# A two-block transformer kernel on one Trainium2 core: its on-chip pools are created in another order, so that the weights and the large tiles start at multiples of 2048 bytes

## The chip, the cores and the metric

The kernel runs on one core of one Trainium2 chip. The core has a matrix engine (TensorE, "PE" in the profile, with its weight loads shown apart as "PEld"), a vector engine (DVE), a scalar engine (ACT), GpSimd (POOL) and SyncE (SP), which here only starts transfers. They work from SBUF, an on-chip memory of 128 partitions; TensorE writes its sums to PSUM. The metric is the device time of one execution in microseconds.

## The reference, cut to what matters

256 tokens of width 1024 pass through two blocks of two layers each. The first block's layer is a gated feed-forward, a mixer of four kinds of attention, and another gated feed-forward; the second block's layer is a mixer of three kinds of attention and one gated feed-forward, with norms that are modulated by a vector c.

```python
def swiglu(h, w_gate, w_up, w_down):
    return (jax.nn.silu(h @ w_gate) * (h @ w_up)) @ w_down

for l in range(DEPTH):                                   # first block
    x = x + 0.5 * swiglu(rms_norm(x, ffn1_norm[l]), ffn1_w_gate[l], ffn1_w_up[l], ffn1_w_down[l])
    h = rms_norm(x, mix_norm[l])
    parts = split_in_proj(h @ w_in[l])
    ...                                                  # o_a, o_b, o_c, o_d: four kinds of attention
    x = x + jnp.concatenate([o_a, o_b, o_c, o_d], axis=-1) @ w_out[l]
    x = x + 0.5 * swiglu(rms_norm(x, ffn2_norm[l]), ffn2_w_gate[l], ffn2_w_up[l], ffn2_w_down[l])

for l in range(DEPTH):                                   # second block
    h = rmsnorm(x, g_mix_pre[l]) * (1.0 + scale_a) + shift_a
    y = hybrid_mixer(h, w_in[l], ...)
    x = x + gate_a * rmsnorm(y, g_mix_post[l])
    h = rmsnorm(x, g_ffn_pre[l]) * (1.0 + scale_f) + shift_f
    x = x + gate_f * rmsnorm(swiglu_2(h, w_gate_up[l], w_down[l]), g_ffn_post[l])
```

Everything is float32, and the large products have to be about that exact.

## The kernel before

**Products in three parts.** A float32 product a·b is made of three products of TensorE's type float32r: a is split into a high and a low part, and so is b, and ah·bh + ah·bl + al·bh is summed in PSUM (`mm3`, line 607). In a product the stationary operand, which a weight load brings into the array first, is 128 tokens of activations (128x128), and the moving operand is 512 columns of the weights (128x512). So every product of 512 columns has a weight load of its own, and three products in a row (a *triple*) make one exact step.

**Weights.** `WStream` (line 378) reads the weights in units of 128x2048 floats (8 KB in each partition): a transfer brings a unit into a tile `raw` (three slots), ACT copies it to `whi` (which rounds it), and DVE subtracts to get `wlo` (four slots each). Both are used once for each of the two tiles of 128 tokens.

**Activations.** `xh` and `xl` hold the transposed, normed input of a phase, 8 KB each in a partition, for the whole phase. The products of the input projections and of gate and up read them as their stationary operand and write the PSUM tile `mm`: in the profile they are `mm<-whi,xh`, `mm<-wlo,xh` and `mm<-whi,xl`. The products of the down projection read the gated middle, transposed and split into `hth` and `htl`, and write the PSUM tiles `y`: `y<-whi,hth`, `y<-wlo,hth`, `y<-whi,htl`. The output projection of a mixer is the same with `oth` and `otl`. These four, and all the small tiles of attention, live in slots of 2 KB of one pool (`m`, line 591, 20 slots). `proj` (line 612) runs through the triples of one `mm` tile, `down` in `ffn` through those of `y`.

**Order.** The program is recorded by `Plan`, and a list schedule with a table of costs sets the order in which each engine takes its instructions. Addresses play no part in that schedule. Every recorded instruction is issued from line 304, so the profile shows one line for nearly all of them, and they are told apart by their tiles.

**Places in SBUF.** A tile pool takes the next free bytes of every partition when it is created, in units of 32 bytes. The pools are created in `Net.__init__`: first `const`, `keep`, `row`, `big` and `sm`, which hold tiles of all sizes, then `mid` (the 2 KB slots), `raw` and `w`. `x`, `xh` and `xl` are tiles of `keep`.

Of the kernel before, what the change touches and what calls it, by code (L numbers as in the profile page):

```python
# [11 lines left out]
F32 = mybir.dt.float32  # L12
F32R = mybir.dt.float32r
# [18 lines left out]
# order of the output projections' (token tile, group of 256 columns); pools of attention's PSUM beside them  # L32
# [3 lines left out]
# engines of the copies out of PSUM, in turn  # L36
COPY = "a"
# the first two units come in CUTS pieces, FIRST of them before the second token tile; up to NCUT in two;
# splits of the others in SPLITS pieces
CUTS, FIRST, NCUT, SPLITS = 4, 2, 5, 2  # L40
# products that warm the array's clock while the first loads are under way
WARM = 8
# the list schedule
# [4 lines left out]
class Pool:  # L48
    """A tile pool whose tiles the plan knows: which slots they share and how many there are."""
# [23 lines left out]
class Plan:  # L73
    """Records the program in its order, then issues it in the order of a list schedule:
    every engine takes, of the instructions whose operands are there, the one needed soonest."""
# [72 lines left out]
    def cost(self, eng, method, args, kw, aps):  # L148
        """ns on the engine, ns on the DMA rings, activation table."""
        if method == "dma_start":  # L150
            return (1000 if eng == "gpsimd" else 475), 4 * int(np.prod(list(args[0].shape))) / 360, None
        n = max(int(np.prod(list(a.shape)[1:])) for k, a in aps)
        psum = any(a.space == PSUM for _, a in aps)
        if eng == "tensor":
            if method == "transpose":
                return 109, 0, None
            n = kw["rhs"].shape[-1]
            if kw["rhs"] is self.cold:
                return 4 * max(107, n / 1.2 + 2), 0, None
            if kw["rhs"].dtype == F32R:  # L160
                return n / 2.4 + 2.5, 0, None
            return 2 * max(107, n / 1.2 + 2), 0, None
        if eng == "scalar":
            extra = 93 * sum(1 for k, _ in aps if k in ("bias", "scale", "accum_out"))
            f = args[2] if len(args) > 2 else kw.get("func")
            return 0.833 * n + (52 if psum else 94) + extra, 0, "silu" if f == AF.Silu else "exp" if f in (AF.Exp, AF.Ln) else None
        if eng == "vector":
            fast = method in ("tensor_copy", "tensor_scalar", "memset") and not psum
            scalars = sum(1 for k, _ in aps if k not in (0, 1, "out", "in_")) if method == "tensor_scalar" else 0
            scalars += sum(1 for k, _ in aps if k == 2) if method == "scalar_tensor_tensor" else 0  # L170
            return n * (0.52 if fast else 1.042) + 68 + 62 * scalars, 0, None
        if eng == "gpsimd":
            if kw.get("op") == ALU.pow:
                return 300 + 165 * n, 0, None
            return 148 + (3.15 if method == "tensor_copy" else 2.11) * n, 0, None
        return 60, 0, None

# [1 line left out]
    def order(self, prio):  # L179
        """List schedule: every engine starts, of what can start within DELTA of the soonest, the most urgent.  # L180
        A tile may take a slot before its turn if the program's order could still go on from there."""
# [41 lines left out]
        def slot_time(i):  # L223
            """When the slots of the tiles that op i touches first are free; None: not now."""
# [81 lines left out]
    def priorities(self):  # L306
        """How long before the end an op has to start, by a schedule from the end; no later than LATE behind
        the large products it was recorded with, and the first loads in their order."""
# [15 lines left out]
    def backward(self, start):  # L324
        """List schedule from the end; a tile waits for the one that had its slot in the program's order."""
# [52 lines left out]
class WStream:  # L378
    """Weights in the order of their use: load ahead, split into hi + lo float32r parts ahead."""
# [9 lines left out]
    def cuts(self, i, n):  # L389
        """The first units come in pieces: the products start the sooner."""  # L390
        k = CUTS if i < 2 else 2 if i < NCUT else 1
        return [slice(j * n // k, (j + 1) * n // k) for j in range(k)]
# [10 lines left out]
    def _load(self, pieces=None):  # L403
        """The next unit, or only the next pieces of it."""
# [47 lines left out]
class Net:  # L452
    def __init__(self, ctx, tc, A, out, stop):
# [3 lines left out]
        pool = lambda name, bufs=1, **k: Pool(nc, ctx.enter_context(tc.tile_pool(name=name, bufs=bufs, **k)), bufs)  # L457
        self.const = pool("const")
        self.keep = pool("keep")
        self.row_p = pool("row", 3)  # L460
        self.big = pool("big", 1)
        self.sm = pool("sm", 4)
        self.mid_p = pool("mid", NMID)
        self.ps = pool("ps", 2, space=PSUM)
        raw_p = pool("raw", 3)
        w_p = pool("w", WStream.BUFS)
        self.ident = self.const.tile([P, P], F32, name="ident")
        self.mhalf = self.const.tile([P, 64], F32, name="mhalf")
        self.x = [self.keep.tile([P, D], F32, name=f"x{t}") for t in range(2)]
        self.xh = self.keep.tile([P, 8, S], F32R, name="xh")  # L470
        self.xl = self.keep.tile([P, 8, S], F32R, name="xl")
# [61 lines left out]
    def rstd2(self, ss):  # L533
        """(ss[0] + ss[1] + eps) ** -0.5: the two halves' parts of a mean of squares."""
# [6 lines left out]
    def norm(self, t, gain, shift=None):  # L541
        """rms_norm(x_t) * gain (+ shift)"""
# [18 lines left out]
    def first_xT(self, t, gain):  # L561
        """xh/xl columns of token tile t := transpose of x_t * gain; the tokens' factors come after the products."""
# [28 lines left out]
    def m(self, n, name, dt=F32):  # L591
        """One of the shared 2 KB slots."""
        return self.mid_p.tile([P, 512], dt, tag="m", name=name)[:, :n]
# [15 lines left out]
    def proj(self, ps, n, t, half, u, kts=4):  # L609
        """ps[128, n] += x^T k-tiles of one weight unit [128, kts, n]."""  # L610
# [125 lines left out]
    def slot(self):  # L736
        """Between the products of a feed-forward: one step of the work that block 2 needs early."""
        if self.bg and next(self.bg[0], self) is self:
            self.bg.pop(0)
# [10 lines left out]
    def copy(self, out, in_):  # L750
        """PSUM -> SBUF, on the engines in turn."""
# [6 lines left out]
    def consts1(self):  # L758
# [4 lines left out]
        self.rope1 = C.tile([P, 2, 176], F32, name="rope1")  # L763
# [15 lines left out]
    def skew(self, name, src, offset, nh, rows, n):  # L779
        """Every head's n values once per row, each row SKEW after the one before: read at SKEW - 1 they slide."""  # L780
# [5 lines left out]
    def diff_lambda(self, l):  # L786
        """-lambda on every partition; the output gain times (1 - lambda_init)."""
# [17 lines left out]
    def na_bias(self, l):  # L805
        """8 * (relative bias, or -1e30 outside the window), [token of a tile, tile, head, key]."""
# [19 lines left out]
    def prep(self, t, ps, segs, w, rope, dstT, flag):  # L826
        """Heads' norms, gains and rotations of a [128, n] projection, then its transpose."""
# [54 lines left out]
    def job(self, kind, l, h, q, k, vh, col, bias=None):  # L882
        """softmax(q k / 8 + bias) v for one head, both token tiles of queries."""
# [32 lines left out]
    def turn_p(self, p):  # L916
        """[query, (tile, key)] -> [key of a tile, (query tile, key tile, query)]"""
# [54 lines left out]
    def turn_o(self, g, flag):  # L972
        """o columns of one group of 256, transposed and split for the output projection."""
# [135 lines left out]
    def modulation(self):  # L1109
        """Rows of block 2's norms: gain * (1 + scale), shift, gate * post gain, twice per layer."""  # L1110
# [52 lines left out]
    def t5_bias(self):  # L1163
        """8 * (table[bucket(q - k)], or -1e30 above the diagonal), keys of the tile before | own tile."""
# [34 lines left out]
    def gated_residual(self, t, y, i):  # L1199
        """x_t += gate * rms_norm(y) * gain"""  # L1200
# [11 lines left out]
    def rot2(self, X, nh, t):  # L1212
        """Rotary positions on [128, nh, 32]."""
# [7 lines left out]
    def latents(self, l, t, ps, st):  # L1221
        """Norms of the latents and their transposes, rotated shared key, forget logits."""
# [27 lines left out]
    def forget(self, l, st):  # L1250
        """F, the cumulative log forget gates: min(z, 0) - log(1 + e), e = exp(-|z|), log(1 + e) = 2 artanh(e / (2 + e)); the fox biases 8 * (F[q] - F[k]), or -1e30 above the diagonal."""
# [26 lines left out]
    def qk_fox(self, t, ps, dst, st):  # L1278
        """Queries [q, 8 F, 1] and keys [k, 1, -8 F], transposed: their products are 8 (q k / 8 + F[q] - F[k])."""
# [32 lines left out]
    def latent_heads(self, t, ps, part, st):  # L1312
        """Four heads of the up-projections: queries (part 0) or keys and values (part 1), transposed."""
# [22 lines left out]
    def causal_job(self, kind, q, k, vh, col, bias, scale):  # L1336
        """Causal softmax(q k * scale + bias) v for one head; bias comes divided by the scale."""
# [30 lines left out]
    def group_norm(self, l, g0, ng):  # L1368
        """rms_norm over groups g0 .. of 256 columns of o, then transposed, times the gain, and split."""
# [188 lines left out]
def pack(inputs):  # L1558
    """Weights laid out as the units are read: every partition's part of a unit is contiguous."""
# [52 lines left out]
def shape_consts():  # L1612
    """Positions, masks and multiplicities: functions of the shapes alone."""
# [51 lines left out]
```

## Time and profile before

| | us |
|---|---|
| three runs | 1671.84, 1675.52, 1676.18 |
| median | 1675.52 |
| span of the profiled execution, first to last instruction | 1670.4 |
| PE busy in it | 1646.5 (99%) |
| PEld, DVE, ACT, POOL busy | 1346.0 (81%), 1086.1 (65%), 841.8 (50%), 166.3 (10%) |

The profiled execution has no time of its own beside its span; the span lies 5.1 us below the median of the three runs. PE's busy time overlaps itself, since matmuls are pipelined: a product of 512 columns is shown as about 0.39 us long, and the next one starts some 0.23 us after it. So what a product costs in a stream is read from the distance between two starts, and not from its length.

### The profile page before, as it was taken

What the parts mean: (1) busy time and instruction counts of PE and PEld (TensorE: products, weight loads), DVE (VectorE), ACT (ScalarE), POOL (GpSimd) and SP (SyncE); (2) the same over time, 40 slices, a digit from 0 to 9 for tenths busy, and PEclk for the clock granted to TensorE, in tenths of its full rate; (3) what the DMA queues carried; (4) which work ended last, traced back from release to release, by engine and by line L of the source; (5) the groups of instructions that cost most, each with busy time, mean ns of one, the idle gap of its engine ahead of it and who ended that gap; (6) DMA issues with size and microseconds to landing.
All of it is one profiled execution on the core that took longest, in us unless ns stands there. A gap on an engine that the chain in (4) does not pass through costs nothing.

```text
span 1670.4 us, 21333 instructions
## 1 busy us (share of the span) xinstructions
PE 1646.5 (99%) x7912; PEld 1346.0 (81%) x7912; DVE 1086.1 (65%) x1956; ACT 841.8 (50%) x1384; POOL 166.3 (10%) x205
## 2 busy tenths in 40 slices
PE   9989999999999999999999999999999999999998
PEld 7868877888888888887788888888888888888886
DVE  6557788577677776777857655656754476585553
ACT  6544456554444444446554444576643358664442
POOL 0000056000000000026500000120000012000000
PEclk9999999999999999998999999999999999999999
DMA  8587762257776877763328645541655445255451
GB/s 302 210 272 274 262 224 102 76 212 298 271 270 250 306 266 268 288 221 121 127 86 316 229 171 192 173 174 51 239 181 199 150 167 202 96 181 190 171 201 51
DMA packets 81884, 335.78 MB, mean 201 GB/s; under 512 B 17136, under 2 KB 19700, under 8 KB 50676
## 3 DMA queue, kind: packets, MB, share of 16 engines
q1 hardware_dynamic: 81780, 334.42, 55.7%
q8 instruction: 62, 1.02, 0.2%
q14 instruction: 42, 0.34, 0.1%
HBM read 333.29 MB, written 2.84 MB: 201 GB/s over the span
## 4 chain that ended last, share of the span: by engine, by line
PE 94%; DVE 2%; POOL 2%; DMA 1%; ACT 1%; issue 0%; SPq 0%; POOLq 0%; DVEq 0%; ACTq 0%
PE mm L304 55%; PE y L304 27%; PE att L304 6%; PE tp L304 6%; DMA raw<-in_gu 1%; POOL rs L304 1%; DVE wlo L304 1%; POOL qk L304 0%; POOL rot L304 0%; DVE o L304 0%; DVE qk L304 0%; DVE ms L304 0%; DMA t5t<-in_t_table 0%; ACT xh L304 0%; DVE qkT L304 0%
## 5 line engine op out<-in xcount | busy, mean ns | idle before, releaser
L304 DVE TENSOR_TENSOR wlo<-raw,whi 128x1024 fp32r<-128x1024 f32 (+2 forms) x516 | 607.5, 1211 | 273.9 <-ACT whi L304 272.4
L304 ACT CAST whi<-raw 128x1024 fp32r<-128x1024 f32 (+2 forms) x516 | 512.5, 1035 | 319.3 <-PE mm L304 132.3
L304 PE MATMUL mm<-whi,xh 128*128 128x512 f32 (+2 forms) x1376 | 552.5, 402 | 2.8 <-ACT whi L304 1.8
L304 PE MATMUL mm<-wlo,xh 128*128 128x512 f32 (+2 forms) x1376 | 543.2, 395 | 0.2 <-DVE wlo L304 0.2
L304 PE MATMUL mm<-whi,xl 128*128 128x512 f32 (+2 forms) x1376 | 539.6, 393 | 0.8 <-DVE xl L304 0.8
L304 PEld LDWEIGHTS mm<-whi,xl 128*128 128x128 f32 x1376 | 259.5, 189 | 61.4 <-DVE xl L304 1.8
L304 PEld LDWEIGHTS mm<-whi,xh 128*128 128x128 f32 x1376 | 259.5, 189 | 61.4 <-ACT whi L304 2.1
L304 PEld LDWEIGHTS mm<-wlo,xh 128*128 128x128 f32 x1376 | 259.7, 189 | 55.3 <-DVE wlo L304 0.9
L304 PE MATMUL y<-whi,htl 128*128 128x512 f32 x528 | 207.5, 393 | 0.0
L304 PE MATMUL y<-wlo,hth 128*128 128x512 f32 x528 | 207.2, 392 | 0.0
L304 PE MATMUL y<-whi,hth 128*128 128x512 f32 x528 | 207.2, 394 | 0.0
L304 ACT ACTIVATE sil<-mm 128x256 f32<-128x256 f32 x110 | 42.3, 384 | 224.1 <-PE mm L304 223.3
L304 POOL TENSOR_TENSOR rs<-rs,mhalf 128x1 f32<-128x1 f32 x28 | 26.1, 932 | 1286.2 <-DVE rs L304 1286.2
L304 DVE CUSTOM_DVE_ANT_0 ada<-ada,act 128x512 f32<-128x512 f32 x192 | 128.7, 691 | 13.5 <-DMA ada<-in_ada 13.2
L304 PEld LDWEIGHTS y<-wlo,hth 128*128 128x128 f32 x528 | 99.7, 189 | 22.7 <-issue 1.3
L304 PEld LDWEIGHTS y<-whi,hth 128*128 128x128 f32 x528 | 99.5, 189 | 21.5 <-ACT whi L304 0.2
L304 PEld LDWEIGHTS y<-whi,htl 128*128 128x128 f32 x528 | 99.7, 189 | 21.3
L304 DVE TENSOR_TENSOR hch<-mm,sil 128x256 f32<-128x256 f32 x110 | 46.4, 421 | 89.7 <-ACT sil L304 89.4
L304 PE MATMUL att<-qkT 64*128 64x256 f32 (+6 forms) x368 | 65.7, 320 | 1.5 <-DVE qkT L304 1.2
L304 POOL TENSOR_TENSOR rs<-ms,mhalf 128x2 f32<-128x2 f32 (+3 forms) x34 | 50.9, 1500 | 136.2 <-DVE ms L304 134.6
L304 PEld LDWEIGHTS att<-V,pt 128*128 128x128 f32 x448 | 58.6, 193 | 6.4 <-ACT pt L304 2.3
L304 PE MATMUL att<-V,pt 128*128 128x65 f32 (+1 forms) x448 | 59.1, 270 | 1.8 <-ACT pt L304 1.8
(158 smaller groups left out, 1390.5 us busy)
## 6 DMA issues: line engine op xcount, KB each, us to landing
raw<-in_gu SPq DMA_DIRECT2D x127, 1024.0 KB, 4.9
raw<-in_dn SPq DMA_DIRECT2D x66, 1024.0 KB, 4.9
ada<-in_ada SPq DMA_DIRECT2D x192, 256.0 KB, 5.3
raw<-in_in SPq DMA_DIRECT2D x32, 1024.0 KB, 4.9
raw<-in_out SPq DMA_DIRECT2D x16, 1024.0 KB, 4.8
row<-moddram SPq DMA_DIRECT2D x12, 512.0 KB, 6.6
raw<-in_in2a SPq DMA_DIRECT2D x4, 840.0 KB, 4.3
raw<-in_gu SPq DMA_DIRECT2D x6, 512.0 KB, 5.8
```

The lines of the kernel that those rows point to most:

```text
L304: getattr(getattr(self.nc, eng), method)(*args, **kw)
```

## The change

The pools are created in another order. A new pool `first` takes `ident` (512 bytes) and `rope1` (1408 bytes, before a tile of `const` that was made later); together with the few constants that lie ahead of it they end at byte 18432, which is nine times 2048. Then come `w`, `raw`, `mid`, a new pool `xT` with `xh`, `xl` and `x`, then `row` and `big`, whose tiles all have sizes that are multiples of 2048 bytes. `const`, `keep` and `sm` come last. No instruction is added, taken away or moved: on each of the five engines the built program has the same instructions in the same order, and each waits for the same semaphores. Comments and docstrings are taken out as well.

```diff
@@ -455,20 +455,24 @@
         self.nc = nc = Plan(tc.nc)
         self.stop = stop
         pool = lambda name, bufs=1, **k: Pool(nc, ctx.enter_context(tc.tile_pool(name=name, bufs=bufs, **k)), bufs)
+
+        first = pool("first")
+        self.ident = first.tile([P, P], F32, name="ident")
+        self.rope1 = first.tile([P, 2, 176], F32, name="rope1")
+        w_p = pool("w", WStream.BUFS)
+        raw_p = pool("raw", 3)
+        self.mid_p = pool("mid", NMID)
+        self.xT = pool("xT")
+        self.xh = self.xT.tile([P, 8, S], F32R, name="xh")
+        self.xl = self.xT.tile([P, 8, S], F32R, name="xl")
+        self.x = [self.xT.tile([P, D], F32, name=f"x{t}") for t in range(2)]
+        self.row_p = pool("row", 3)
+        self.big = pool("big", 1)
         self.const = pool("const")
         self.keep = pool("keep")
-        self.row_p = pool("row", 3)
-        self.big = pool("big", 1)
         self.sm = pool("sm", 4)
-        self.mid_p = pool("mid", NMID)
         self.ps = pool("ps", 2, space=PSUM)
-        raw_p = pool("raw", 3)
-        w_p = pool("w", WStream.BUFS)
-        self.ident = self.const.tile([P, P], F32, name="ident")
         self.mhalf = self.const.tile([P, 64], F32, name="mhalf")
-        self.x = [self.keep.tile([P, D], F32, name=f"x{t}") for t in range(2)]
-        self.xh = self.keep.tile([P, 8, S], F32R, name="xh")
-        self.xl = self.keep.tile([P, 8, S], F32R, name="xl")
         self.W = WStream(nc, raw_p, w_p, self.unit_specs())
...
@@ -760,7 +764,6 @@
         C = self.const
         for _ in range(6):
             yield
-        self.rope1 = C.tile([P, 2, 176], F32, name="rope1")
         nc.sync.dma_start(self.rope1, A["c_rope1"])
```

The start of the large tiles within a partition, from the two built programs:

| tile | bytes | before: start | past a multiple of 2048 | past a multiple of 64 | after: past a multiple of 2048 |
|---|---|---|---|---|---|
| `whi`, `wlo` (4 slots each) | 8192 | 161472 on | 1728 | 0 | 0 |
| `raw` (3 slots) | 8192 | 136896 on | 1728 | 0 | 0 |
| 2 KB slots (`hth`, `htl`, `oth`, `otl`, ...) | 2048 | 95936 on | 1728 | 0 | 0 |
| `xh`, `xl` | 8192 | 46944, 55136 | 1888 | 32 | 0 |
| `x` (2) | 4096 | 38752, 42848 | 1888 | 32 | 0 |
| `row` (3), `hn`/`o` of `big` | 4096, 8192 | 71648, 83936 | 2016 | 32 | 0 |
| `ident` | 512 | 16512 | 128 | 0 | 128 |

A stationary tile of 128 columns takes 512 bytes of such a tile, a moving one of 512 columns takes 2048.

## Rows read from the trace of the kernel before

**Rows 1.** The page, parts 1 and 2: busy time; clock granted to TensorE.

```profile
PE 1646.5 (99%) x7912; PEld 1346.0 (81%) x7912; DVE 1086.1 (65%) x1956; ACT 841.8 (50%) x1384; POOL 166.3 (10%) x205
PEclk9999999999999999998999999999999999999999
```

**Rows 2.** The chain that ended last: shares; then pieces, with start, us, engine, tile, count.

```profile
by line: PE mm L304 54.7%; PE y L304 26.9%; PE att L304 6.0%; PE tp L304 5.9%; DMA raw<-in_gu 1.2%; POOL rs L304 0.9%; DVE wlo L304 0.7%; POOL qk L304 0.5%; POOL rot L304 0.4%; issue 0.4%; DVE o L304 0.3%; DVE qk L304 0.2%; DVE ms L304 0.2%
...
69.01 5.51 PE y L304 x24
...
430.31 5.61 PE mm L304 x24
...
524.75 10.91 PE y L304 x48
...
709.87 16.38 PE y L304 x72
```

**Rows 3.** Groups of PE by shape: count, busy us, mean ns, idle before.

```profile
L304 PE MATMUL mm<-whi,xh 128*128 128x512 f32 x1312 | 531.2, 405 | 2.6 <-ACT whi L304 1.8 <-ACT xh L304 0.7
...
L304 PE MATMUL y<-whi,htl 128*128 128x512 f32 x528 | 207.5, 393 | 0.0
...
L304 PE MATMUL y<-wlo,oth 128*128 128x512 f32 x128 | 51.2, 400 | 0.0
```

**Rows 4.** PE's timeline in a run of `mm` products: start us, length us.

```profile
431.32 0.39 PE L304 MATMUL mm<-whi,xl 128*128 128x512 f32 x1
...
434.12 0.39 PE L304 MATMUL mm<-whi,xl 128*128 128x512 f32 x1
```

**Rows 5.** PE's timeline in a run of `y` products.

```profile
339.57 0.39 PE L304 MATMUL y<-wlo,oth 128*128 128x512 f32 x1
339.80 0.39 PE L304 MATMUL y<-whi,otl 128*128 128x512 f32 x1
...
342.29 0.39 PE L304 MATMUL y<-wlo,oth 128*128 128x512 f32 x1
```

**Rows 6.** Two stretches (`mm`, then `y`): busy of each engine, PEclk, DMA share, GB/s.

```profile
430.31:435.92 5.61, 5.61 (x27) 4.46 (x26) 3.66 (x6) 2.00 (x2) 0.00 (x0) 1.00 0.89 323
409.84:412.79 2.95, 2.95 (x15) 2.44 (x14) 2.95 (x6) 0.15 (x1) 0.00 (x0) 1.00 0.87 347
```

**Rows 7.** PE's timeline where a run of `y` follows a run of `mm`.

```profile
407.52 0.40 PE L304 MATMUL y<-whi,hth 128*128 128x512 f32 x1
...
409.61 0.39 PE L304 MATMUL y<-whi,hth 128*128 128x512 f32 x1
```

**Rows 8.** PE's timeline, `mm` of 420 columns: the first product of three triples.

```profile
1065.58 0.35 PE L304 MATMUL mm<-whi,xh 128*128 128x420 f32 x1
...
1066.16 0.35 PE L304 MATMUL mm<-whi,xh 128*128 128x420 f32 x1
...
1066.73 0.35 PE L304 MATMUL mm<-whi,xh 128*128 128x420 f32 x1
...
1067.31 0.35 PE L304 MATMUL mm<-whi,xh 128*128 128x420 f32 x1
```

**Rows 9.** PE's timeline, `mm` of 256 columns: first and last of thirteen products.

```profile
300.27 0.28 PE L304 MATMUL mm<-whi,xh 128*128 128x256 f32 x1
...
301.71 0.28 PE L304 MATMUL mm<-whi,xh 128*128 128x256 f32 x1
```

**Rows 10.** Groups of PE by shape: transposes of two kinds of tiles.

```profile
L304 PE MATMUL tp<-ident,hch 128*128 128x128 f32 x264 | 39.1, 273 | 0.0
...
L304 PE MATMUL tp<-ident,hn 128*128 128x128 f32 x144 | 20.1, 272 | 0.0
```

**Rows 11.** Groups of DVE by shape, 512 columns.

```profile
L304 DVE TENSOR_TENSOR hn<-x,row 128x512 f32<-128x512 f32 x16 | 10.8, 685 | 0.4
...
L304 DVE TENSOR_TENSOR wlo<-raw,whi 128x512 fp32r<-128x512 f32 x12 | 8.1, 687 | 3.4 <-ACT whi L304 3.2
```

**Rows 12.** The chain that ended last: its longest piece that is a transfer.

```profile
78.02 14.39 DMA raw<-in_gu
```

## The prediction

> **What bounds the kernel now.** I read the page first. TensorE is busy for 1646.5 of 1670.4 us, no other engine for more than 65% (its weight loads run beside its products), and the clock granted to it is at its upper level, 2.4 GHz, nearly throughout [rows 1]. The chain that ended last says the same: 81.6% of the span are products of the two large kinds, `mm` (54.7%) and `y` (26.9%); all DVE, ACT, POOL and transfer steps together are a few per cent [rows 2]. So the question is what one large product costs. The groups by shape give the counts: `mm` has three kinds of 1312 products of 512 columns, 3936 in all; `y` has three kinds of 528 and three of 128, 1968 in all [rows 3]. Their mean lengths, 393 to 405 ns, are of no use, because products overlap. The timeline has what is needed, the distance between starts. In a run of `mm`, twelve products lie between 431.32 and 434.12 us: 2.80 us, 233.3 ns each [rows 4]. In a run of `y`, twelve lie between 339.57 and 342.29: 2.72 us, 226.7 ns each [rows 5]. That is the observation on which everything below rests: same number of columns, same type, same weights in the same slots, same clock, and yet `mm` takes 6.6 ns more.
>
> What can make that difference? Not the load on the memory by others: `y` keeps 2.95 us for 13 products (226.9 ns) in a stretch in which DVE is busy without a break and transfers move 347 GB/s, while `mm` takes 5.61 us for 24 (233.8 ns) at 323 GB/s and less DVE [rows 6]. The clock is 1.00 in both. The moving operand is the same in both, a quarter of `whi` or `wlo`. What differs is the stationary operand: `xh` and `xl` start 32 bytes past a multiple of 64, `hth`, `htl`, `oth` and `otl` on one. I take this as the likely cause: a weight load off such a multiple takes more from the product that runs above it.
>
> **The change, part by part.** *Instructions, order, waits:* the same, so they give nothing by themselves. What is left is placement.
>
> *`xh` and `xl` (32 past a multiple of 64, then 0).* The trace doesn't show `mm` of 512 columns with an aligned stationary tile in a settled run; the nearest row is `y`, which differs from it in nothing else that I can find in the operands. From above: 6.6 ns on each of 3936 products, 26.0 us. From below I use runs as they really stand, because `y` needs some products to settle: behind a run of `mm`, its first nine products take from 407.52 to 409.61 us, 232.2 ns each [rows 7]. A piece of 24 `y` products is 5.51 us long, a piece of 24 `mm` 5.61 us; 48 and 72 `y` are 10.91 and 16.38 us, 227.3 and 227.5 ns each [rows 2]. If every `mm` run were as short as 24 and settled as slowly, the gain would be 0.10 us per 24, 4.2 ns each: 16.4 us. The `mm` runs are longer than 24 as often as not, and some products stand behind small attention products and don't run in a stream, so I take 20 us, a little under the middle of 16.4 and 26.0.
>
> *Narrower `mm` products.* Those of 420 columns take 1.73 us for nine, 192.2 ns [rows 8], those of 256 columns 1.44 us for twelve, 120.0 ns [rows 9]. Counted at one column per cycle of 2.4 GHz, the columns alone are 175.0 and 106.7 ns, which leaves 17.2 and 13.3 ns; for 512 columns it leaves 20.0 in `mm` and 13.4 in `y`. So at 256 columns there is nothing to win, at 420 some 3.8 ns on 96 products, 0.4 us: inside my rounding.
>
> *The moving operand (1728 past a multiple of 2048, then 0).* The 420-column products are a test that the kernel makes by itself: their moving tiles start 0, 16, 32 and 48 bytes past a multiple of 64, one triple after the other, and the triples take 0.58, 0.57 and 0.58 us [rows 8]. At this grain the moving start does not matter. For a coarser grain (256 or 2048) no row speaks, since all moving tiles of 512 columns stand at 1728 now. The bounds are nothing and all of the 13.4 and 20.0 ns above the columns alone, 26.4 + 78.7 = 105.1 us; I take nothing, the value of the nearest row.
>
> *The 2 KB slots (1728, then 0), stationary for `y`.* A multiple of 64 before and after: nothing, by the same reasoning. But if `mm` takes up `y`'s rhythm, the nine slow products at the head of a `y` run may go: 50 ns for each of 48 runs (six feed-forwards, seven `y` runs between gate-and-up products and one at the end), at most 2.4 us. I leave it out of the sum.
>
> *`x`, `row`, `hn` (1888 and 2016, then 0).* Two operands of DVE at different starts, `x` and `row`, take 685 ns; two at the same start, `raw` and `whi`, 687 ns for the same 512 columns [rows 11]. Placement is nothing to DVE. TensorE's transposes read `hn` off a multiple of 64 and `hch` on one, and both are 272 or 273 ns long [rows 10]: nothing there either, in products that are not float32r.
>
> *Where the saved time goes.* The one long piece of the chain that is not TensorE's is a transfer of 14.39 us [rows 12]; it stays as it is, and the products that run beside it save nothing there: 0.9% of the span, so 0.2 us of the 20. Elsewhere DVE, with 35% of the span idle [rows 1], and the transfers keep the weights ahead: before `mm`'s first kind PE stands idle for 2.6 us in all [rows 3].
>
> *The sum.* 1670.4 - 20 = 1650.4 us of span. Applied to the median, from which the span lies 5.1 us: 1675.5 - 20 = **1655.5 us**. With the bounds of this case, 16.4 and 26.0 + 0.4 + 2.4 = 28.8 us, it lies between 1646 and 1660.
>
> **A rule that speaks against it.** The rows say that a product's price depends on which stationary tile is loaded under it: 226.7 or 233.3 ns [rows 4, 5]. The Trainium skill's page "TensorE: Matmul & The Clock Gate", section "Step-by-step: what each phase is for", says that moving operand and weight load have read ports of their own, so that loading the next weights takes no read bandwidth from the running product. By that rule where the stationary tile starts costs nothing, and this change would leave 1675.5 us. The trace does not agree as far as two kinds of products differ, but it does not show that the start is the reason.
>
> **The rivals.** *B, the start is not the cause.* `mm` also differs from `y` in its use of PSUM: a run of `mm` adds up in one tile, while `y` changes tiles after each triple. If that sets 233.3 ns, nothing changes: 1675.5 us, within 5 us. Against it: inside a `y` triple three products add to one tile too, and I see no step at the change of tiles. For it: no row isolates the start, and the transposes are indifferent [rows 10].
>
> *C, more than `mm` gains.* If the grain is coarser than 64 bytes, moving and stationary starts at multiples of 2048 help both kinds. At most all of 105.1 us goes, 1570 us; with half, 53 us, 1623 us. For it: 13.4 ns above the columns are in `y` too, and no row says from what. Against it: the indifferent 420-column triples. The Trainium skill's page "TensorE: Matmul & The Clock Gate", section "Back-to-back issue gap", gives about 216 ns for 512 columns in a warm stream; an estimate from it is 17.3 x 3936 + 10.7 x 1968 ns = 89 us less, 1586 us.
>
> *D, slower.* Now every stationary and moving tile starts on the same phase of 2048 bytes. If a load and a stream that start together get in each other's way, `y` falls to the rhythm of `mm`: 6.6 ns on 1968 products, 13.0 us, 1688.5 us. It decides as soon as closeness of phase outweighs the multiple of 64. Against it: `y`'s stationary tiles already lie whole multiples of 512 bytes from its moving ones, as all will, and they are the quick ones.
>
> **How the numbers follow.** A (`mm` takes `y`'s rhythm) 0.54; B 0.22; C 0.14; D 0.10. The time is that of A, 1655.5 us. To hold eight times in ten the range takes in A and B and the weaker half of C: 1622 to 1679 us. It leaves out D and the strong half of C. About 0.3%, 5 us, is what three runs of this kernel can tell from no change. Faster by more: A and C and a sliver of B, 0.69; within: 0.21; slower: 0.10.
>
> **What would show it.** In the changed kernel the timeline of an `mm` run should have twelve products in about 2.72 us, a piece of 24 in the chain about 5.45 to 5.51 us; `y` runs 2.72 us per twelve as now; DVE's 512-column rows 685 to 687 ns; and the chain's share of `mm` smaller by about a hundredth. `mm` still at 2.80 us is B. Both kinds under 2.70 us is C. `y` above 2.75 us is D. The prediction would also go wrong if `mm` got quicker and the time did not follow: then PE's idle time before `mm`, now 2.6 us [rows 3], would grow behind ACT or DVE.

## The result, and the profile after

The changed kernel takes 1653.0 us (median of four runs, 1649.27 to 1655.27) and the kernel before 1673.96 us in four runs beside it: a ratio of 0.987 with a 95% interval of 0.9852 to 0.9888, 21 us less. The forecast was 1655.5 us, 20 us less. The time and the quick `mm` came as forecast; the reason that the prediction gave for them did not hold, as the experiments show.

The page of the changed kernel, whose profiled execution took 1654.43 us, first the span, then parts 1 and 2:

```profile
span 1652.7 us, 21333 instructions
...
PE 1627.0 (98%) x7912; PEld 1347.2 (82%) x7912; DVE 1085.4 (66%) x1956; ACT 842.3 (51%) x1384; POOL 167.9 (10%) x205
...
PEclk9989999999999999998899999999999999999999
```

Against [rows 1], PE is busy 19.5 us less and nothing else has moved by more than 2 us. The chain that ended last, shares and then pieces (start, us, engine, tile, count):

```profile
by line: PE mm L304 53.7%; PE y L304 26.6%; PE att L304 6.1%; PE tp L304 5.9%; DMA raw<-in_gu 1.3%; DVE wlo L304 1.1%; POOL rs L304 1.1%; issue 0.6%; POOL qk L304 0.5%; POOL rot L304 0.4%; DVE o L304 0.3%; DVE qk L304 0.2%; DVE ms L304 0.2%
...
76.30 14.11 DMA raw<-in_gu
...
355.94 16.64 PE mm L304 x72
...
457.55 5.44 PE mm L304 x24
463.43 5.49 PE mm L304 x24
...
1033.42 16.39 PE y L304 x72
```

`mm` has lost one hundredth of the span, as the prediction asked. A piece of 24 `mm` takes 5.44 or 5.49 us (5.61 in [rows 2]), 72 of them 16.64 us; 72 `y` take 16.39 us, as before. The transfer that nothing hides is 14.11 us long ([rows 12] 14.39). In the timeline of PE (start, length) thirteen products of a run of `mm`, then thirteen of a run of `y`:

```profile
350.81 0.39 PE L304 MATMUL mm<-wlo,xh 128*128 128x512 f32 x1
351.03 0.39 PE L304 MATMUL mm<-whi,xl 128*128 128x512 f32 x1
351.26 0.39 PE L304 MATMUL mm<-whi,xh 128*128 128x512 f32 x1
...
353.53 0.39 PE L304 MATMUL mm<-wlo,xh 128*128 128x512 f32 x1
```

```profile
334.94 0.39 PE L304 MATMUL y<-wlo,oth 128*128 128x512 f32 x1
...
337.66 0.39 PE L304 MATMUL y<-wlo,oth 128*128 128x512 f32 x1
```

From the first to the last are twelve distances, 2.72 us in both, 226.7 ns each: `mm` had 233.3 ns in [rows 4] and now has the rhythm that `y` had in [rows 5]. The groups by shape, of PE and then of DVE (count, busy us, mean ns, idle before):

```profile
L304 PE MATMUL mm<-whi,xh 128*128 128x512 f32 x1312 | 525.7, 401 | 2.2 <-ACT whi L304 1.5 <-ACT xh L304 0.7
```

```profile
L304 DVE TENSOR_TENSOR hn<-x,row 128x512 f32<-128x512 f32 x16 | 10.8, 684 | 0.4
...
L304 DVE TENSOR_TENSOR wlo<-raw,whi 128x512 fp32r<-128x512 f32 x12 | 8.1, 689 | 2.8 <-ACT whi L304 2.6
```

PE waits before the first kind of `mm` for 2.2 us in all (2.6 in [rows 3]), so the weights still keep ahead; DVE's rows are those of [rows 11] within 2 ns.

**Where the time came from.** Summed over the trace, the distances from one 512-column `mm` product to the next start (those under 260 ns; a longer one holds a wait or a lower clock) fell from 877.0 us (3759 of them) to 852.9 us (3743), and those of `y` from 433.1 to 430.6 us. As the counts show, the sums of `mm` do not hold the same products. Taken product by product, the 3739 `mm` distances that are under 260 ns in both traces lost 20.3 us, and the 1895 of `y` 2.2 us. The other 221 distances behind `mm` products, longer in one trace or in both, grew by 4.8 us. What is left is the 17.7 us between the two spans. Part of the growth is the clock. Windows of the same piece of work, first of the kernel before, then of the changed one (start and end, length, busy of PE, PEld, DVE, ACT and POOL with counts, PEclk, DMA share, GB/s):

```profile
800.00:812.00 12.00, 10.18 (x60) 7.73 (x59) 10.82 (x33) 4.40 (x11) 9.24 (x9) 1.00 0.48 170
812.00:822.00 10.00, 10.00 (x59) 8.15 (x58) 6.71 (x16) 6.41 (x13) 3.07 (x3) 1.00 0.05 11
```

```profile
790.00:802.00 12.00, 10.15 (x56) 8.04 (x55) 9.82 (x33) 4.85 (x12) 8.56 (x8) 0.91 0.52 175
802.00:812.00 10.00, 10.00 (x39) 7.76 (x38) 3.60 (x13) 3.74 (x8) 2.59 (x3) 0.60 0.00 0
```

In both PE stood idle for about 1.8 of 12 us in the first stretch. Before, the clock stayed at 2.4 GHz; in this execution of the changed kernel it was at its lower level, 1.2 GHz, for most of the next 10 us, and 39 products were done there in place of 59. By an estimate from that row, a mean clock of 0.60 for 10 us costs about 4 us. Of the fourteen traces of this document, nine show the lower clock at these products, two (the kernels with the 160-byte pad below) some 50 products earlier, and three at neither place. The four spans of the changed kernel, 1647.5 to 1653.5 us, have mean clocks of 0.992 to 0.988.

### The profile page after: what moved, and what is told of

Read it like the earlier page. It is cut to its first block, busy times and chain, and to the rows that moved or that the text cites. A ratio compares the mean times of both kernels' runs of the same rounds, so it can differ in the third digit from the quotient of the medians.

```text
span 1652.7 us, 21333 instructions
## 1 busy us (share of the span) xinstructions
PE 1627.0 (98%) x7912; PEld 1347.2 (82%) x7912; DVE 1085.4 (66%) x1956; ACT 842.3 (51%) x1384; POOL 167.9 (10%) x205
## 4 chain that ended last, share of the span: by engine, by line
PE 92%; DVE 3%; POOL 2%; DMA 1%; issue 1%; ACT 1%; SPq 0%; POOLq 0%; DVEq 0%; ACTq 0%
PE mm L304 54%; PE y L304 27%; PE att L304 6%; PE tp L304 6%; DMA raw<-in_gu 1%; DVE wlo L304 1%; POOL rs L304 1%; POOL qk L304 0%; POOL rot L304 0%; DVE o L304 0%; DVE qk L304 0%; DVE ms L304 0%; DVE xl L304 0%; SPq L304 0%; DMA t5t<-in_t_table 0%
## 5 line engine op out<-in xcount | busy, mean ns | idle before, releaser
L304 PE MATMUL mm<-whi,xh 128*128 128x512 f32 (+2 forms) x1376 | 547.0, 398 | 2.5 <-ACT whi L304 1.5
L304 PE MATMUL mm<-wlo,xh 128*128 128x512 f32 (+2 forms) x1376 | 537.3, 391 | 0.7 <-DVE wlo L304 0.7
```

Of the source, the lines that this page charges most:

```text
L304: getattr(getattr(self.nc, eng), method)(*args, **kw)
```

## The experiments

For each run I worked out the address of each operand from the built program. By **distance** I mean the start of the stationary tile less that of the moving tile of the same product, in bytes; since one stationary tile lies 512 bytes from the next and one moving tile 2048, it has one value modulo 512 for all 512-column products of a kind. By **pitch** I mean the mean distance in time between two starts, from the tenth product of a run on (some 2420 values for `mm`, 1250 for `y` in each trace). Before, `mm` has distance 1888 - 1728 = 160 and `y` 0. All experiments move tiles by idle padding or by the order of pools; the instructions, their order and waits are those of the kernel before.

### One placement at a time

`e1_xh_only`: the kernel before, with `xh` and `xl` on a multiple of 64.

```diff
+        self.keep.tile([P, 8], F32, name="pad0")
         self.xh = self.keep.tile([P, 8, S], F32R, name="xh")
         self.xl = self.keep.tile([P, 8, S], F32R, name="xl")
+        self.keep.tile([P, 8], F32, name="pad1")
```

> The kernel before with nothing changed but xh and xl, which move up by 32 bytes to a multiple of 64 (1920 past a multiple of 2048); all that lies behind them moves by 64 bytes, so the weights and the 2 KB slots stay on multiples of 64 and off multiples of 2048. Theory A (what counts is that the stationary tile starts on a multiple of 64): all of the gain, 1650 to 1656 us, twelve mm products in 2.72 us. Theory M (multiples of 2048, or the moving operand): nothing, 1670 to 1678 us, mm at 2.80 us per twelve.

`e2_xh_off`: the changed kernel, with the same two pads around `xh` and `xl` in `xT`, which puts these two alone 32 bytes further.

> The changed kernel with xh and xl alone 32 bytes past a multiple of 64; everything else stays on multiples of 64, the weights and the 2 KB slots on multiples of 2048. Theory A: the gain is gone, 1671 to 1677 us, mm at 233.3 ns, y at 226.7 ns. Theory M: 1650 to 1656 us.

`e3_slots_off`: the changed kernel, with the 2 KB slots 32 bytes further (and what follows them, `xh` and `xl` too, 64).

```diff
+        pool("pad_a").tile([P, 8], F32, name="pad0")
         self.mid_p = pool("mid", NMID)
+        pool("pad_b").tile([P, 8], F32, name="pad1")
```

> The changed kernel with the 2 KB slots (hth, htl, oth, otl and attention's tiles) 32 bytes past a multiple of 64, xh and xl 64 past a multiple of 2048. Theory A: mm keeps 226.7 ns, y takes 233.3 ns: 6.6 ns on 1968 products, 13 us more, about 1666 us (1660 to 1670). Theory M, or a cause in how mm and y use PSUM: no change, 1650 to 1656 us.

`e4_weights_off`: the changed kernel, with the same two pads around the pool `w`: `whi` and `wlo` 32 bytes further, everything behind them 64.

> The changed kernel with whi and wlo, the moving operands, 32 bytes past a multiple of 64; xh, xl and the 2 KB slots 64 past a multiple of 2048. Theory A (the stationary tile's own start): no change, 1650 to 1656 us. Theory D (what counts is the distance between the starts of stationary and moving tiles): mm and y both at 233.3 ns, 6.6 ns on 5904 products, 39 us more, about 1690 us. Theory M: slower by some part of that.

Measured, with before at 1673.76 us (26 runs): e1 1669.59 us, 0.9974 (0.9963 to 0.9985); e2 1670.38, 0.9984 (0.9971 to 0.9997); e3 1680.33, 1.0046 (1.0028 to 1.0064); e4 1679.93, 1.0036 (1.0021 to 1.005). The chain's pieces of 72 `mm` and 36 `y`, first one of the kernel before, then those of e1 and of e3:

```profile
551.62 17.06 PE mm L304 x72
```

```profile
510.27 8.20 PE y L304 x36
551.31 17.05 PE mm L304 x72
```

```profile
514.20 8.40 PE y L304 x36
555.91 17.06 PE mm L304 x72
714.91 16.79 PE y L304 x72
```

e1 contradicts the prediction: `xh` on a multiple of 64 leaves `mm` where it was, 17.05 us against 17.06. In e3 the stationary tiles of `mm` lie on a multiple of 64 too, and `mm` is slow; `y`, whose slots alone are off, is now slow as well. e4 is the sharpest. There no activation has left its multiple of 64, only the weights are 32 bytes off, and the timeline shows both kinds slow:

```profile
356.68 0.40 PE L304 MATMUL mm<-wlo,xh 128*128 128x512 f32 x1
...
359.48 0.40 PE L304 MATMUL mm<-wlo,xh 128*128 128x512 f32 x1
```

```profile
339.72 0.40 PE L304 MATMUL y<-whi,oth 128*128 128x512 f32 x1
...
342.52 0.40 PE L304 MATMUL y<-wlo,oth 128*128 128x512 f32 x1
```

Twelve distances take 2.80 us in both, 233.3 ns. So neither tile's own start decides. What the slow cases share is that the two starts differ: by 160 before, 128 in e1, 32 in e2, 64 and 32 in e3, 32 and 32 in e4. Rival B falls here also: these runs leave PSUM alone and move the pitch from 226.8 to 233.3 ns and back. The times follow: `mm` is slow in e2 and in e3, `y` only in e3. Product by product, the times to the next start that are under 260 ns in both add up to 10.8 us more in e3 for `y` and to 0.3 us more for `mm`; the medians lie 10.0 us apart. Two forecasts of time failed all the same: e3 was expected at 1660 to 1670 us and e4 at about 1690, and both came to 1680. And e1 and e2 are 4.2 and 3.4 us faster than before, clear of the noise, with a slow `mm`; such sums for `mm` and `y` together account for 2.5 and 2.4 us of that, and the rest is not explained.

### Distance alone

`e5_pad160`: if only distance counts, the kernel before needs one idle tile of 160 bytes and no new order. Everything behind it then lies 1888 past a multiple of 2048, off every multiple of 64, as `xh` and `xl` do.

```diff
         self.xl = self.keep.tile([P, 8, S], F32R, name="xl")
+        self.keep.tile([P, 40], F32, name="pad")
```

> The kernel before with one idle tile of 160 bytes behind xl. Everything behind it moves by 160, so xh, xl, the 2 KB slots, whi and wlo all start 1888 past a multiple of 2048: none on a multiple of 64, and every stationary tile a multiple of 512 away from its moving one. Theory R (what counts is that the distance between the starts of the stationary and the moving tile is a multiple of 512, wherever both lie): mm and y both 226.7 ns, 1649 to 1657 us. Theory A (the stationary start on a multiple of 64) and theory S (multiples of 2048): mm and y both 233.3 ns, 1687 us.

It took 1653.45 us (1651.19 to 1656.35), 0.9877 (0.9858 to 0.9896), the time of the change. Its chain, and thirteen `y` products of its timeline:

```profile
505.52 8.16 PE y L304 x36
546.24 16.62 PE mm L304 x72
```

```profile
339.64 0.39 PE L304 MATMUL y<-whi,otl 128*128 128x512 f32 x1
...
342.36 0.39 PE L304 MATMUL y<-whi,otl 128*128 128x512 f32 x1
```

Both kinds have the quick rhythm (2.72 us for twelve), with not one stationary or moving tile on a multiple of 64. That takes the last support from the multiple of 64, and from the multiple of 2048 too.

`e8_xl_only`: the changed kernel with one pad between `xh` and `xl` and one behind `xl`; only every third product of `mm` has a distance of 32.

> The changed kernel with xl alone 32 bytes off, xh on the weights' phase: one of three weight loads of each mm triple is off. If each load costs for itself: mm at 226.7 + 6.6 / 3 = 228.9 ns, about 1661 us. If one load that is off upsets the whole run: mm at 233 ns, about 1671 us.

1672.35 us (one run). The run of `mm` is slow in the mean, 2.79 us for twelve products, with `y` untouched (5.45 us for 24):

```profile
366.76 0.40 PE L304 MATMUL mm<-whi,xh 128*128 128x512 f32 x1
...
367.69 0.40 PE L304 MATMUL mm<-wlo,xh 128*128 128x512 f32 x1
367.93 0.39 PE L304 MATMUL mm<-whi,xl 128*128 128x512 f32 x1
368.15 0.40 PE L304 MATMUL mm<-whi,xh 128*128 128x512 f32 x1
...
369.55 0.40 PE L304 MATMUL mm<-whi,xh 128*128 128x512 f32 x1
```

The mean pitch, 233.4 ns, is no smaller than with all three off, so one displaced load of three does not cost a third. Within a triple the price is spread unevenly. The mean time is 238.9 ns from the start of `wlo,xh` to that of `whi,xl`, the displaced one, 228.5 ns from there to `whi,xh`, and 232.4 ns to the next `wlo,xh`; with all three off (e2) they are 233.1 to 233.5 ns. Moving one of the two halves buys nothing.

### How coarse is the grain

Four more kernels put other distances in place. The edit is in the order of pools and the sizes of pads, always behind `first`: e6 `w, raw, pad 192, xT, pad 64, mid`; e9 the same with pads of 224 and 64; e7 `mid, pad 96, xT, pad 32, w, raw`, which makes the distances negative; e10 the same with pads of 64 and 192. The lines of e6 and of e10:

```diff
         raw_p = pool("raw", 3)
-        self.mid_p = pool("mid", NMID)
+        pool("pad_a").tile([P, 48], F32, name="pad0")
         self.xT = pool("xT")
...
         self.x = [self.xT.tile([P, D], F32, name=f"x{t}") for t in range(2)]
+        pool("pad_b").tile([P, 16], F32, name="pad1")
+        self.mid_p = pool("mid", NMID)
```

```diff
-        w_p = pool("w", WStream.BUFS)
-        raw_p = pool("raw", 3)
         self.mid_p = pool("mid", NMID)
+        pool("pad_a").tile([P, 16], F32, name="pad0")
         self.xT = pool("xT")
...
+        pool("pad_b").tile([P, 48], F32, name="pad1")
+        w_p = pool("w", WStream.BUFS)
+        raw_p = pool("raw", 3)
```

> The changed kernel with xh and xl 192 and the 2 KB slots 256 bytes past the weights' multiple of 2048, everything on a multiple of 64. Theory R with 512 as the step: mm and y both at 233 ns, about 1680 us as with the slots off. Theory R with 256 as the step: mm 233 ns, y 226.7 ns, about 1670 us. Theory A: both 226.7 ns.

> The changed kernel with the weights behind the other pools: xh and xl start 32, the 2 KB slots 128 bytes short of the weights' phase (all distances up to now were on the other side). Theory R: mm and y both at 233 ns, about 1680 us. If only stationary starts ahead of the moving phase cost something: both 226.7 ns, 1650 to 1656 us.

> The changed kernel with xh and xl 224 and the 2 KB slots 288 bytes past the weights' phase: both 32 off from 256, the distance at which y was quick, on either side. Theory R with a step of 256: mm and y both at 233 ns, as at a distance of 32, about 1680 us. If there is a broad quick range about 256 (a distance of 192 gave 229.1 ns): mm under 229 ns, y near 226.7 ns, 1653 to 1659 us.

> The changed kernel with the weights behind the other pools: xh and xl start 192, the 2 KB slots 256 bytes short of the weights' phase. If distances count in steps of 512: -256 is as 256, y 226.7 ns, and -192 is as 320, 64 beyond 256; with a range that lies evenly about 256, mm at 229 ns, about 1657 us. If the range reaches on one side of 256 only: mm at 233 ns, about 1670 us.

All values together, with the pitch worked out as said above:

| kernel | `mm` distance | `mm` pitch, ns | `y` distance | `y` pitch, ns | us |
|---|---|---|---|---|---|
| before | 160 | 233.2 | 0 | 227.1 | 1673.96 |
| the change | 0 | 226.8 | 0 | 226.8 | 1653.0 |
| e1 | 128 | 232.7 | 0 | 227.0 | 1669.59 |
| e2 | 32 | 233.3 | 0 | 227.0 | 1670.38 |
| e3 | 64 | 233.2 | 32 | 233.2 | 1680.33 |
| e4 | 32 | 233.3 | 32 | 233.3 | 1679.93 |
| e5 | 0 | 226.8 | 0 | 226.7 | 1653.45 |
| e6 | 192 | 229.1 | 256 | 226.7 | 1657.4 (one run) |
| e7 | -32 | 233.3 | -128 | 232.8 | 1684.44 (one run) |
| e8 | 0, `xl` 32 | 233.4 | 0 | 226.8 | 1672.35 (one run) |
| e9 | 224 | 233.2 | 288 | 233.2 | 1684.2 (one run) |
| e10 | -192 | 233.3 | -256 | 226.7 | 1669.83 (one run) |

Chain pieces of e9 and of e10, where `y` is slow and quick, and PE's timeline of e6, twelve distances of `mm`:

```profile
513.06 8.39 PE y L304 x36
554.75 17.06 PE mm L304 x72
```

```profile
510.42 8.19 PE y L304 x36
551.48 17.07 PE mm L304 x72
```

```profile
356.82 0.39 PE L304 MATMUL mm<-whi,xh 128*128 128x512 f32 x1
...
359.57 0.39 PE L304 MATMUL mm<-whi,xh 128*128 128x512 f32 x1
```

0, 256 and -256 are quick; 32, 64, 128, 160, 224, 288, -32, -128 and -192 are slow. So the grain is 256 bytes, for all values but one: at 192 `mm` in e6 takes 2.75 us for twelve, 229.2 ns, between the two. -192, which is 64 modulo 256, is fully slow, as 64 itself is. I have no explanation for 192.

### Once more, side by side

`e11_pad160_again` and `e12_change_again` are e5 and the changed kernel again, on one chip, to see whether the order of pools gives anything beyond the distance.

> The kernel before with the one idle tile of 160 bytes once more, as a second timing: 1649 to 1657 us, the changed kernel's time.

> The changed kernel beside it on the same chip: the same time as the kernel with the idle tile, within 3 us, if the distance is all that the change does.

The pad takes 1648.99 us (1646.23 to 1654.64), 0.9861 (0.9834 to 0.9887); the change 1650.17 us (1646.46 to 1656.84), 0.9861 (0.9832 to 0.9891); before is at 1674.47 us (7 runs). They are equal, and no kernel here beats them. The window of e12 from 802 to 812 us, then that of e11 from 780 to 792 us:

```profile
802.00:812.00 10.00, 8.29 (x29) 6.47 (x30) 4.83 (x19) 4.22 (x9) 4.52 (x6) 0.66 0.25 99
```

```profile
780.00:792.00 12.00, 10.95 (x39) 7.46 (x37) 12.00 (x38) 5.01 (x10) 10.39 (x10) 0.73 0.42 147
```

Both dipped in their profiled executions, 0.66 and 0.73, some 50 products apart; from 780 to 820 us both have a mean clock of 0.91. Nothing here makes the dip a property of the order of pools, and the medians show no difference.

## Why the prediction came out as it did

**`mm` takes `y`'s rhythm: right.** 226.7 ns in place of 233.3, and 20.3 us over the 3739 `mm` products whose next start follows in under 260 ns in both traces: within the bounds of 16.4 and 26.0, and what the 20 us taken said. The heads of the `y` runs, bounded at 2.4 us and left out, did come: -2.2 us. A piece of 24 `y` fell from 5.50 us to 5.44 on the mean of 34 pieces. They do not need a quick `mm`: e2, with `mm` slow, has 5.45.

**The saved time stays saved: partly.** The prediction gave back 0.2 us for products beside a transfer. In the profiled execution 4.8 us came back in longer distances, part of it in the stretch at 1.2 GHz. 20.3 and 2.2 us less that are the 17.7 us of the two spans; the medians differ by 21. So two terms that the forecast's 20 leaves out, 2.2 us more and 4.8 us less, cancel in part, and that it lies so close to the 21 us of the medians owes something to that.

**The cause: wrong.** The step that failed is "a weight load off such a multiple takes more from the product that runs above it". The multiple of 64 was what the quick and the slow kind of before differed in, but they differed in distance too, 0 and 160, and I did not separate the two. e4 (stationary tiles on multiples of 64: slow) and e5 (none on one: quick) do. That the gain came in spite of the wrong cause is luck: the change that put `xh` and `xl` on a multiple of 64 also made their distance from the weights 0. e1, which does only what the prediction's cause asks for, gains 4.2 us in place of 20.

**"At this grain the moving start does not matter": wrong, and it hid the cause.** The test was the triples of 420 columns [rows 8]. Their moving tiles lie 1680 bytes apart, so in the kernel before their distances modulo 256 are 160, 16, 128 and 240: none is 0. Nor are they alike: in nanoseconds of that trace the triples take 568 to 572 at 16 and 240 and 576 to 586 at 160 and 128, which 0.58, 0.57 and 0.58 us hide. In the changed kernel they are 0, 112, 224 and 80. Five triples of its timeline, first products:

```profile
1053.27 0.35 PE L304 MATMUL mm<-whi,xh 128*128 128x420 f32 x1
...
1053.83 0.36 PE L304 MATMUL mm<-whi,xh 128*128 128x420 f32 x1
...
1054.40 0.35 PE L304 MATMUL mm<-whi,xh 128*128 128x420 f32 x1
...
1054.97 0.35 PE L304 MATMUL mm<-whi,xh 128*128 128x420 f32 x1
...
1055.55 0.35 PE L304 MATMUL mm<-whi,xh 128*128 128x420 f32 x1
```

The first, at distance 0, takes 0.56 us, the others 0.57 or 0.58. In nanoseconds of the trace the two triples at 0 in this run take 560 and 563, the five others 569 to 579. e5, whose distances are the same, has 560 and 563 against 569 to 579. It is a second sign of the same rule, within one run, in another shape, though of few values. The triples of the other kernels (`xh` and `xl` moved together) add the remaining multiples of 16: 565 to 567 ns at 0 in e2 and e4, 565 to 568 at 192 in e6, e7 and e9, 565 to 583 at 224, and 570 to 586 at all others but 16, among them 578 and 579 at 96 in e1. So 192 stands out here too.

**The rivals.** B fell with e2 to e4. D named the right quantity, the phase of load and stream to each other, with the wrong sign: starting together is what is quick. The remark against D, that `y`'s tiles lie whole multiples of 512 bytes apart and are quick, was the answer, and I used it only to lower D. C asked for less than 226.7 ns; no distance tried gives that at 512 columns. The 216 ns behind C's 1586 us is, in the section of the Trainium skill's page that the prediction names, the gap of an isolated product (another section has it for products back to back); the quickest here is 226.7 ns. What the 13.4 ns above the columns alone consist of stays open.

**The rule that speaks against it.** The Trainium skill's page "TensorE: Matmul & The Clock Gate", section "Step-by-step: what each phase is for", says that loading the next weights takes no read bandwidth from the running product. In these runs the same loads beside the same products make a pitch of 226.7 or 233.3 ns by relative start alone. So they do meet somewhere. Where was not shown: banks or lines of the memory, or the way that the two requests are lined up, would all be stories.

**Left open.** Why 256 bytes; the middle value at 192; why one displaced load of three costs as much as three; 96 modulo 256 at 512 columns, which was not tried, and there steps finer than the 32 bytes that pools allow. Products of 256 columns do not follow the rule: the 84 of them in each trace whose next start follows in under 140 ns have a mean pitch of 119.5 ns at a distance of 0 (the change) and of 115.8 and 115.2 ns at 64 and -192 (e3 and e10).

## What to carry to other kernels

When streams of the same shape run at two rhythms, list the starts of *both* operands and their difference before naming one; here float32r products of 512 columns cost 226.7 ns when the stationary and the moving tile start a multiple of 256 bytes apart, 229.1 ns at 192, and 232.7 to 233.4 ns at the nine other distances tried. One idle tile of 160 bytes can be worth 1.2% of a kernel that TensorE bounds, and it is cheaper than a new order of pools. A test that a kernel makes by itself, such as the four starts of the 420-column tiles, is only a test if one of its values is in the quick class and if it is read finely enough.

## What the runs showed of the hardware that was not expected

- The price of a float32r product of 512 columns depends on where its two SBUF operands lie to each other, modulo 256 bytes, and not on where either lies: 226.7 to 227.1 ns at 0, 256 and -256, 232.7 to 233.4 ns at nine other distances, 229.1 ns at 192.
- One displaced stationary tile of three costs as much in the mean as three, 233.4 ns, but unevenly: 238.9, 228.5 and 232.4 ns within a triple (e8).
- After the same idle time, 1.8 of 12 us, TensorE's clock was 1.00 in the profiled execution of the kernel before and 0.60 in that of the changed one for the next 10 us; among the runs of one kernel mean clocks of 0.988 to 0.992 go with spans 6 us apart.
